# Later and paced first solve step, spread fetches of the compression weights, and a transposition by matmul, in a hybrid attention and RWKV-7 layer

## The chip, the core and the metric

The kernel runs on one core of a Trainium2 chip. The metric is the device time of one execution in microseconds (us). The kernel before takes 551.33 us, the median of 3 runs (551.25 to 551.44).

Five instruction streams run side by side, each in its own order: TensorE (PE, matmuls, with its weight loads as PEld), VectorE (DVE), ScalarE (ACT), GpSimd (POOL) and SyncE (SP), which here only issues DMA transfers. An instruction that waits for a semaphore holds up everything behind it on its engine.

## What is computed

One decoder layer for 256 tokens of width 2048. A normalised input goes through one wide projection, whose columns feed two groups of heads: eight heads of sparse attention (NSA) and sixteen heads of RWKV-7 (a recurrence over time with a 64x64 state per head). Both outputs are gated and go through one output projection. Cut to its frame, the reference reads:

```python
h      = rms_norm(x, pre_norm_g) @ w_in          # one projection, split by columns
kc     = compress(k_cmp, pos_k, k_w1, k_w2)      # 15 blocks of 32 tokens
vc     = compress(v_cmp, pos_v, v_w1, v_w2)
o_c    = softmax(q @ kc + bias) @ vc             # compressed branch
o_s, o_w                                         # selected and windowed branches
attn   = g0 * o_c + g1 * o_s + g2 * o_w
# RWKV-7, for every head and token
sa     = state @ a_t
state  = state * w_t + sa * b_t + v_t * k_t
y_t    = state @ r_t
out    = x + rms_norm((concat(attn * silu(za), y * silu(zb))) @ w_out)

def compress(kv, pos, w1, w2):
    flat = (blocks of 32 tokens of kv) + pos     # 32 x 128 = 4096 wide
    return silu(flat @ w1) @ w2
```

The layer is computed in float32 accuracy: each weight is split into a high and a low part of type f32r, a float32 that TensorE takes at a higher rate than plain float32.

## The kernel before

**Pieces.** The projection is cut into pieces of 128 output columns, which the main loop goes through one by one (L1251 and below). A piece j consists of two halves of 512 KB of weights. `load_raw` (L314) has SP fetch a half into one of four buffers; `cast` makes the high part on ACT (L322) and the low part on DVE (L323). Tiles carry the piece and the half: `rf170` is the raw first half of piece 17, `hf170` its high part and `lf170` its low part. (The profile leaves the number out and shows a serial number: `hf__1431` is `hf170`, `lf__1430` is `lf170`, `hf__1481` is `hf171`.) PE multiplies a half in 16 matmuls with the high part and 8 with the low one, all through the helper at L171. A weight buffer comes free when its cast is done, so a cast that is late on DVE holds up SP's next fetch and every DMA behind it.

**Order.** A planner in Python decides the order. Work beside the projection runs in lanes of generators; a `yield x` asks to go on x us of estimated PE time later. Tiles of SBUF come from a pool of 66 units (`arena`), PSUM from `banks`. Then the instructions are laid out by priority, and each engine runs in order. `pace(ins, to)` makes an instruction wait for a matmul on the chip; `behind` only fixes an order. `marks` holds the last matmul after each piece, so `marks[-1]` is the one after the newest piece.

**The RWKV solve** (`solve`, L805) runs once for each half of the RWKV heads. Four DMAs (L816) gather a matrix from the tile GR, which DVE writes at L779, into DRAM (`us`), and one DMA (L822) loads it as U. Then 31 steps on DVE follow, each a multiplication (L829) and an addition (L831), the first at `j == 31`.

**The compression** (`compress`, L1029) runs for the keys (kc) and the values (vc). Its first weight matrix, cw1, comes in eight parts of 512 KB, four for each; `fetch_cw` (L1020) takes four arena units for a part and has SP fetch it (L1026). Eight small fp32 matmuls use a part. DVE copies the sum out of PSUM (`csb`, L1061), and a small matmul of 32 columns on that copy (L1064) adds up the four 32-row groups. An activation and a second small product follow.

**The input for the later pieces** comes once more: `stage` loads the input in two transfers of 1 MB (L526) and scales it in eight DVE instructions each (L529).

**An attention head** (`nsa_head`, L1091) turns its probabilities by PE: six transpositions of 128x128 and two of the small tile `lcs` (L1164), all through the helper at L200 with the fp32 identity.

Of the kernel before, what the change touches and what calls it, by code (L numbers as in the profile page):

```python
# [11 lines left out]
F32 = mybir.dt.float32  # L12
F32R = mybir.dt.float32r
AF = mybir.ActivationFunctionType
ALU = mybir.AluOpType

P = 128
# [119 lines left out]
def hybrid_block(ctx: ExitStack, tc: tile.TileContext, xT, xtok, wfm, wtm, wout, vecs, gpost, lora, table,  # L137
# [28 lines left out]
    def mm(o, lhsT, rhs, **kw):  # L166
        n = 1
        for d_ in rhs.shape[1:]:
            n *= d_
        now[0] += n * (1 if rhs.dtype == F32R else 4) / 2400.0  # L170
        last[0] = PE.matmul(o, lhsT, rhs, **kw)  # L171

    last = [None]
# [24 lines left out]
    def transpose(o, i, idn):  # L198
        now[0] += 0.11
        PE.transpose(out=o, in_=i, identity=idn)  # L200
# [21 lines left out]
    def bank():  # L222
        while banks.find(1) is None:
            yield lambda: banks.find(1) is not None
        return banks.take(1)
# [210 lines left out]
    marks = []  # L436
# [45 lines left out]
    cmat = cst[:, K_CM:K_CM + P]  # L482
    bonr = cp.tile([P, P], F32R, name="bonr")
    ACT.activation(bonr, bones, AF.Copy)
    gmask = cst[:, K_GM:K_GM + P]
    qsum = cst[:, K_Q:K_Q + 32]
    smask = cst[:, K_SM:K_SM + T]
# [317 lines left out]
    def solve(hb):  # L805
# [16 lines left out]
        SP.dma_start(U, us)  # L822
        POOL.memset(Z, 0.0)
        POOL.memset(Zs[0:64, 0:1024:33], 1.0)
        yield 5.0
        for j in range(31, 0, -1):
            w = 32 - j
            t_ = tmp[0:64, 0:j * w].rearrange("p (s t) -> p s t", s=j)
            DVE.tensor_tensor(t_, U[:, 0:j, j:j + 1].to_broadcast([64, j, w]),  # L829
                              Z[:, j:j + 1, j:32].to_broadcast([64, j, w]), op=ALU.mult)  # L830
            DVE.tensor_tensor(Z[:, 0:j, j:32], Z[:, 0:j, j:32], t_, op=ALU.add)  # L831
            if hb == 0 or j % 2:
                yield ZLAT
# [195 lines left out]
    def compress(a, nm):  # L1029
        if a == 0:  # L1030
            pace(SP.dma_start(post, pos), marks[-2])
            pace(SP.dma_start(w2t, cw2), marks[-2])
            fetch_cw(2, False)
        blks = yield from sb(4)
        blk = blks.ap.rearrange("p (j g i) -> p j g i", j=32, g=2)
        POOL.memset(blk[:, :, :, 15:16], 0.0)
        src = cT[nm].ap
        for g in range(2):
            w_g = bass.AP(tensor=src.tensor, offset=src.offset + g * T, ap=[src.ap[0], [1, 32], [16, 15]])
            DVE.tensor_tensor(blk[:, :, g, 0:15], w_g, post[:, a, :, None].to_broadcast([P, 32, 15]), op=ALU.add)  # L1040
        cT[nm].free(2.0)
        yield 1.0
        cps = yield from bank()
        for hf in range(4):
            n = 4 * a + hf
            fetch_cw(min(n + 3, 8), False)
            if n not in cws:
                yield lambda: arena.find(4) is not None
                fetch_cw(n + 1, True)
                yield 4.0  # L1050
            w1 = cws.pop(n)
            for j in range(2):
                for q in range(4):
                    jj = 4 * j + q
                    mm(cps[32 * q:32 * q + 32, 0:P], blk[:, 8 * hf + jj].rearrange("p g i -> p (g i)"),
                       w1[:, jj * P:jj * P + P], start=hf == 0 and j == 0, stop=hf == 3 and j == 1)
            w1.free(1.0)
            yield CWLAT
        blks.free(1.0)
        csb = yield from sb()  # L1060
        DVE.tensor_copy(csb[:, 0:P], cps[:, 0:P])  # L1061
        cps.free(1.0)
        yps = yield from bank()
        mm(yps[:, 0:32], csb[:, 0:P], qsum, start=True, stop=True)  # L1064
        csb.free(1.0)
        yh = tp.tile([P, 32], F32, tag="yh", name=f"yh{nm}")
        DVE.tensor_scalar(yh, yps[:, 0:32], 0.5, None, op0=ALU.mult)
        yps.free(1.0)
        yt = tp.tile([P, 32], F32, tag="yt", name=f"yt{nm}")
        ACT.activation(yt, yh, AF.Tanh)  # L1070
        DVE.scalar_tensor_tensor(yh, yt, 1.0, yh, op0=ALU.add, op1=ALU.mult)
        yield 2.0
        ops = yield from bank()
        if a == 0:
            mm(ops[:, 0:32], w2t[:, a, :], yh, start=True, stop=True)
            for g in range(2):
                ACT.activation(KCH[:, g, 128:144], ops[:, 16 * g:16 * g + 16], AF.Copy)
                DVE.tensor_tensor(KCL[:, g, 128:144], ops[:, 16 * g:16 * g + 16], KCH[:, g, 128:144].bitcast(F32),
                                  op=ALU.subtract)
        else:  # L1080
            for g in range(2):
                mm(ops[0:16, g * P:(g + 1) * P], yh[:, 16 * g:16 * g + 16], w2t[:, a, :], start=True, stop=True)
            opv = ops[0:16, 0:2 * P].rearrange("p (g d) -> p g d", g=2)
            ACT.activation(vcS[0:16], opv, AF.Copy)
            ACT.activation(vcS[64:80], opv, AF.Copy)
            DVE.tensor_tensor(vcS[32:48], opv, vcS[0:16].bitcast(F32), op=ALU.subtract)
        ops.free(2.0)
        ready_kv[nm] = True
        yield 0.4

    def nsa_head(h, qts):  # L1091
# [70 lines left out]
        for j in range(6):  # L1162
            transpose(ptf[:, j * P:(j + 1) * P], lg[:, j * P:(j + 1) * P], ident)
        for i in range(2):  # L1164
            transpose(ctp[0:80, i * P:(i + 1) * P], lcs[:, i, :].bitcast(F32), ident)
        pT = lg
        cTt = tp.tile([P, T], F32R, tag="hr", name=f"cTt{h}", bufs=NHR)
        ACT.activation(cTt[0:80], ctp[0:80, 0:T], AF.Copy)
# [82 lines left out]
    for j, (nm, i) in enumerate(FM):  # L1251
        if j == N_PRE_TM:
            token_major()
        if j == N_SWITCH - 6:
            lanes["stage"].append(stage())
        until(lambda: arena.find(4) is not None)
        pt = proj(j)
        if j == 0:
            row_statistics()
        A = halves[i // 4] if nm in ("k", "r", "v") else None  # L1260
        if nm == "wa":
            wa = pick(arena, 1)
            shifted(pt, j, 24, wa[:])
            rw.append(wa_split(wa))
        elif nm == "k":
            h2 = (i % 4) // 2
            if i % 2 == 0:
                A.pair[h2] = pick(arena, 4)
                pv = A.pair[h2].ap.rearrange("p (a b t) -> p a b t", a=2, b=2)
                for q in range(2):  # L1270
                    A.ks[i % 4 + q], A.nrm[i % 4 + q] = pv[:, 0, q], pv[:, 1, q]
                A.left = getattr(A, "left", [2, 2])
            shifted(pt, j, i, A.ks[i % 4])
            rw.append(k_norm(A, i % 4, i))
            if i % 2 == 1:
                rw.append(k_ready(A, i % 4 - 1))
                if i % 4 == 1:
                    rw.append(begin(i // 4))
                for q in (i - 1, i):
                    lanes[f"blk{q % 2}"].append(block(A, i // 4, q % 4, q))  # L1280
        elif nm in ("r", "v"):
            o = pick(arena, 1)
            shifted(pt, j, (8 if nm == "r" else 16) + i, o[:])
            (A.r if nm == "r" else A.v)[i % 4] = o
        elif nm in ("kc", "vc"):
            if i == 0:
                cT[nm] = pick(arena, 2)
            with at("evac"):
                evacuate(cT[nm][:, i * T:i * T + T], pt, j)
            if i == 1:  # L1290
                lanes["nsa0"].append(compress(("kc", "vc").index(nm), nm))
        elif nm in ("ks", "kw"):
            kt = fbuf[turn[0] % 2][:, 1:T + 1]
            with at("evac"):
                evacuate(kt, pt, j)
            for o, w in ((slice(0, 128), slice(0, 128)), (slice(400, 528), slice(128, 256))) if nm == "ks" else (
                    (slice(144, 400), slice(0, 256)),):
                ACT.activation(KCH[:, i, o], kt[:, w], AF.Copy)
                DVE.tensor_tensor(KCL[:, i, o], kt[:, w], KCH[:, i, o].bitcast(F32), op=ALU.subtract)
        elif nm == "q":  # L1300
            qt = pick(arena, 1)
            with at("evac"):
                evacuate(qt[:], pt, j, SCALE)
            lanes[f"nsa{i % NL}"].append(nsa_head(i, qt))
        else:
            if i == 0:
                zt_ = rp.tile([P, 8 if nm == "za" else 4, T], F32, tag="lorS" if nm == "za" else "waS", name="all" + nm)
            if nm == "za" or i < 4:
                z = Kept(zt_[:, i, :])
            else:  # L1310
                z = pick(arena, 1)
            with at("evac"):
                evacuate(z[:], pt, j, 0.5)
            lanes["gate"].append(silu(i + (8 if nm == "zb" else 0), z))
            if nm == "zb":
                gates.append((i, z))
# [184 lines left out]
```

## Time and profile before

| quantity | value |
|---|---|
| median of 3 runs | 551.33 us |
| the profiled execution's own time | 553.0 us |
| span from its first to its last instruction | 551.2 us |
| mean TensorE clock granted in it | 0.994 |
| DVE, ACT, POOL busy in the span | 427.4, 312.2, 55.7 us |
| bytes moved | 101.98 MB, 185 GB/s on average |

Times in the rows of the profile count from the first instruction of the span. A row of the timeline holds its start, its length to the end of the last instruction in the group, engine, line, operation, tiles (written <- read), the count and, in brackets, the idle time before it and what ended it. Matmuls are pipelined, so the spacing of the starts tells what one costs, and the length of a single one does not. A plain fp32 matmul leaves two records.

### The profile page before, as it was taken

How to read it: one execution, taken by the hardware profiler on the slowest of the kernel's cores; microseconds unless marked ns; L12 is line 12 of the kernel's file. 1: busy time of each engine (PE TensorE's matmuls, PEld its weight loads, DVE VectorE, ACT ScalarE, POOL GpSimd, SP SyncE). 2: the span in 40 equal slices, each digit the busy share in tenths (PEclk: the TensorE clock that was granted, in tenths of full speed). 3: DMA queues.
4: the chain of work that ended last, by engine and by line, in shares of the span. 5: the costliest groups of instructions: out<-in, count | busy, mean ns of one | idle time of the engine just before them, and what ended most of it. 6: DMA issues, size and time to landing. Idle time of an engine off the chain costs nothing.

```text
span 551.2 us, 10942 instructions
## 1 busy us (share of the span) xinstructions
PE 541.9 (98%) x4208; PEld 483.8 (88%) x4208; DVE 427.4 (78%) x862; ACT 312.2 (57%) x595; POOL 55.7 (10%) x101
## 2 busy tenths in 40 slices
PE   9999999999999999999999999999999999999995
PEld 8999999989988888888998888988988887888884
DVE  5888999869989877556699969999776753776654
ACT  6858665432746554443766868758764434754532
POOL 3202433000000000000532101000000000000000
PEclk9999999998999999999999999999999999999998
DMA  8957444888555575433456464444642446847524
GB/s 298 386 186 262 142 156 155 316 267 319 168 187 182 189 223 182 141 107 99 117 184 203 132 175 141 149 156 134 183 131 86 155 165 205 317 154 230 190 77 152
DMA packets 41167, 101.98 MB, mean 185 GB/s; under 512 B 14203, under 2 KB 16412, under 8 KB 40476
## 3 DMA queue, kind: packets, MB, share of 16 engines
q1 hardware_dynamic: 40828, 100.98, 55.4%
q8 instruction: 33, 0.54, 0.4%
q10 hardware_dynamic: 288, 0.31, 0.2%
q14 instruction: 18, 0.15, 0.1%
HBM read 96.03 MB, written 5.24 MB: 184 GB/s over the span
## 4 chain that ended last, share of the span: by engine, by line
PE 88%; DMA 5%; ACT 2%; DVE 2%; SPq 1%; issue 1%; POOL 0%; DVEq 0%; ACTq 0%
PE banks L171 86%; PE banks L200 2%; DMA xr<-in_xT_dram 1%; DMA arena<-us 1%; DMA us<-GR 1%; DMA rf__3422<-in_wfm_dram 1%; DMA rf__95<-in_wfm_dram 1%; SPq L816 1%; ACT xs L397 0%; POOL arena L713 0%; ACT arena L499 0%; DVE arena L999 0%; ACT L712 0%; DVE GR L779 0%; DVE arena L733 0%
## 5 line engine op out<-in xcount | busy, mean ns | idle before, releaser
L171 PE MATMUL banks<-arena 128*32 128x128 f32 (+3 forms) x470 | 30.2, 253 | 1.1 <-POOL arena L304 1.1
L171 PEld LDWEIGHTS banks<-arena 128*32 128x32 f32 (+3 forms) x470 | 25.7, 136 | 4.5 <-POOL arena L304 1.1
L829 DVE TENSOR_TENSOR arena<-arena 64x31 f32<-64x31 f32 (+15 forms) x62 | 20.4, 329 | 5.2 <-DMA arena<-us 4.5
L831 DVE TENSOR_TENSOR arena<-arena 64x31 f32<-64x31 f32 (+15 forms) x62 | 20.3, 328 | 0.6
L633 ACT ACTIVATE small<-small 128x256 f32<-128x256 f32 x25 | 12.5, 502 | 10.7 <-DVE small L619 7.1
L618 ACT ACTIVATE small<-banks 128x256 f32<-128x256 f32 x37 | 13.9, 375 | 4.4 <-PE banks L171 4.3
L200 PE MATMUL banks<-small,arena 128*128 128x128 f32 x96 | 14.7, 274 | 0.0
L634 DVE SCALAR_TENSOR_TENSOR arena<-small 128x256 f32<-128x256 f32 x25 | 11.8, 476 | 3.6 <-ACT small L633 3.5
L678 DVE RECIPROCAL arena<-banks 128x256 f32<-128x256 f32 x8 | 13.8, 1740 | 0.8 <-PE banks L171 0.8
L1140 ACT ACTIVATE arena<-arena,mx 128x128 f32<-128x128 f32 (+1 forms) x32 | 14.1, 443 | 0.0
L171 PE MATMUL banks<-VS,GR 128*64 128x64 f32 x256 | 13.6, 228 | 0.0
L171 PEld LDWEIGHTS banks<-VS,GR 128*64 128x64 f32 x256 | 10.9, 137 | 1.5 <-issue 0.4
L713 POOL TENSOR_SCALAR arena<-arena 128x256 f32<-128x256 f32 x8 | 9.5, 1189 | 26.1 <-ACT arena L712 26.1
L952 POOL MEMSET arena<- 64x256 f32 x12 | 3.7, 308 | 83.4 <-DVE arena L634 28.8
L200 PEld LDWEIGHTS banks<-small,arena 128*128 128x128 f32 x96 | 11.2, 140 | 1.0
L779 DVE TENSOR_TENSOR GR<-banks,small 128x1024 f32<-128x1024 f32 x8 | 9.7, 1212 | 2.9 <-PE banks L171 2.9
L926 DVE COPY VS<-banks 64x512 f32<-64x512 f32 x8 | 5.5, 687 | 7.5 <-PE banks L171 7.5
L956 POOL TENSOR_TENSOR arena<-arena,PC 128x256 f32<-128x256 f32 x4 | 3.3, 836 | 78.7 <-DVE arena L946 49.7
L732 POOL TENSOR_SCALAR AR<-arena,small 128x4 f32<-128x4 f32 x8 | 7.4, 932 | 31.8 <-DVE arena L634 31.8
L1136 DVE CUSTOM_DVE_ANT_0 arena<-banks,arena 128x128 f32<-128x128 f32 (+1 forms) x32 | 10.0, 349 | 0.0
L171 PE MATMUL banks<-AR,arena 64*128 64x128 f32 x128 | 9.3, 285 | 0.0
L171 PEld LDWEIGHTS banks<-AR,arena 64*128 64x128 f32 x128 | 7.8, 187 | 1.5 <-issue 0.7
(1165 smaller groups left out, 1780.5 us busy)
## 6 DMA issues: line engine op xcount, KB each, us to landing
arena<-in_cw_dram SPq DMA_DIRECT2D x8, 512.0 KB, 8.2
arena<-in_wfm_dram SPq DMA_DIRECT2D x4, 512.0 KB, 8.6
arena<-in_xT_dram SPq DMA_DIRECT2D x2, 1024.0 KB, 7.5
xres<-in_xtok_dram SPq DMA_DIRECT2D x2, 1024.0 KB, 5.7
out_dram<-y SPq DMA_DIRECT2D x7, 256.0 KB, 2.4
xr<-in_xT_dram SPq DMA_DIRECT2D x3, 512.0 KB, 7.2
bscr<-arena SPq DMA_DIRECT2D x1, 1536.0 KB, 7.5
arena<-bscr SPq DMA_DIRECT2D x8, 128.0 KB, 2.9
```

The source lines that it names most:

```text
L171: last[0] = PE.matmul(o, lhsT, rhs, **kw)
L200: PE.transpose(out=o, in_=i, identity=idn)
L618: ACT.activation(t, pt[:, T:2 * T], AF.Copy, scale=scale)
L633: ACT.activation(tm, f[:, 0:T], AF.Copy, scale=vcol(V_MU, c))
L634: DVE.scalar_tensor_tensor(o, f[:, 1:T + 1], omu[:, c:c + 1], tm, op0=ALU.mult, op1=ALU.add)
L678: DVE.reciprocal(A.nrm[i], sp[:, :T])
L713: POOL.tensor_scalar(u[:], u[:], 1.0, None, op0=ALU.add)
L779: DVE.tensor_tensor(A.GR[:, i].rearrange("p h c t -> p (h c) t"), gp.ap.rearrange("p h (c t) -> p (h c) t", c=4), gmask[:, None, :].to_bro ...
L829: DVE.tensor_tensor(t_, U[:, 0:j, j:j + 1].to_broadcast([64, j, w]), Z[:, j:j + 1, j:32].to_broadcast([64, j, w]), op=ALU.mult)
L831: DVE.tensor_tensor(Z[:, 0:j, j:32], Z[:, 0:j, j:32], t_, op=ALU.add)
L1136: DVE.tensor_tensor_reduce(out=dst, in0=src, in1=bb, scale=1.0, scalar=-3.0e38, op0=ALU.add, op1=ALU.max, accum_out=mx[:, i, j:j + 1])
L1140: ACT.activation(dst, dst, AF.Exp, bias=mx[:, i, j:j + 1], accum_out=sm[:, i, j:j + 1])
```

## The change

The change has five parts.

- `idr`, a copy of the 128x128 identity of type f32r, is made once by ACT.
- In `solve` the planner is asked for 10 instead of 5 us of PE time before the loop, and the first multiplication of the loop is paced on `marks[-1]`.
- In `compress` the planner lets 2.5 us pass between the copy `csb` and the small matmul, and that matmul is ordered behind `marks[-1]`.
- In `nsa_head` the two transpositions of `lcs` (16 in all) become f32r matmuls with `idr` as the moving side, 128 columns each.
- At the pieces 8 to 16 the loop fetches one part of cw1 a piece, where at least 24 units of the arena are free.

```diff
+    idr = cp.tile([P, P], F32R, name="idr")
+    ACT.activation(idr, ident, AF.Copy)
@@ solve
-        yield 5.0
+        yield 10.0
         for j in range(31, 0, -1):
             w = 32 - j
             t_ = tmp[0:64, 0:j * w].rearrange("p (s t) -> p s t", s=j)
-            DVE.tensor_tensor(t_, U[:, 0:j, j:j + 1].to_broadcast([64, j, w]),
-                              Z[:, j:j + 1, j:32].to_broadcast([64, j, w]), op=ALU.mult)
+            step_ = DVE.tensor_tensor(t_, U[:, 0:j, j:j + 1].to_broadcast([64, j, w]),
+                                      Z[:, j:j + 1, j:32].to_broadcast([64, j, w]), op=ALU.mult)
+            if j == 31:
+                pace(step_, marks[-1])
@@ compress
         csb = yield from sb()
         DVE.tensor_copy(csb[:, 0:P], cps[:, 0:P])
         cps.free(1.0)
+        yield 2.5
         yps = yield from bank()
         mm(yps[:, 0:32], csb[:, 0:P], qsum, start=True, stop=True)
+        behind(last[0], marks[-1])
@@ nsa_head
         for i in range(2):
-            transpose(ctp[0:80, i * P:(i + 1) * P], lcs[:, i, :].bitcast(F32), ident)
+            mm(ctp[0:80, i * P:(i + 1) * P], lcs[:, i, :], idr, start=True, stop=True)
@@ loop over the pieces
+        if 8 <= j < 17 and arena.busy.count(False) >= 24:
+            fetch_cw(cwn[0] + 1, True)
```

What this does to the order of the instructions shows at three places. In the changed kernel the lines move by 2 to 8: L779 becomes L781, L816 L818, L822 L824, L829 L831, L831 L835, L1026 L1030 and L1061 L1065.

SP, before, from the fetch of three parts of cw1 to the one of the last two; `GR0`, `us0` belong to the first solve:

```order
L1026 DMA arena_73<-in_cw1_dram 128x1024 x3
L314 DMA rf170__1428<-in_wfm_dram 128x1024
L526 DMA arena_73<-in_xT_dram 128x2048
L314 DMA rf171__1478<-in_wfm_dram 128x1024
L1026 DMA arena_73<-in_cw1_dram 128x1024 x2
L816 DMA us0_1459<-GR0_675 32x16x32 x3
L314 DMA rf180__1521<-in_wfm_dram 128x1024
L816 DMA us0_1459<-GR0_675 32x16x32
L314 DMA rf190__1567<-in_wfm_dram 128x1024
L822 DMA arena_73<-us0_1459 64x1024
```

All eight parts are fetched here and in the four rows behind. The same stretch of SP in the changed kernel is without them; two come later, the last one here:

```order
L528 DMA arena_73<-in_xT_dram 128x2048
L314 DMA rf170__1434<-in_wfm_dram 128x1024
L314 DMA rf171__1483<-in_wfm_dram 128x1024
L818 DMA us0_1465<-GR0_677 32x16x32 x3
L314 DMA rf180__1523<-in_wfm_dram 128x1024
L818 DMA us0_1465<-GR0_677 32x16x32
...
L314 DMA rf211__1839<-in_wfm_dram 128x1024
L314 DMA rf220__1873<-in_wfm_dram 128x1024
L1030 DMA arena_73<-in_cw1_dram 128x1024
```

Six of the eight parts now stand ahead of these rows, between the fetches of the pieces 10 and 15. The first 1 MB of the second input stands ahead of piece 17. The eighth part of cw1 stands behind the fetch of `rf220`, which waits until DVE has cast `lf200`.

DVE, before, around the first step of the first solve (L829); L529 scales the second input, L1061 copies the compression's sum:

```order
L323 TENSOR_TENSOR lf170__1430<-rf170__1428,hf170__1431 128x1024
L616 SCALAR_TENSOR_TENSOR arena_73<-banks_74,small_72 128x256
L323 TENSOR_TENSOR lf171__1480<-rf171__1478,hf171__1481 128x1024
L1040 TENSOR_TENSOR arena_73<-arena_73,small_72 128x32x15
L829 TENSOR_TENSOR arena_73<-arena_73 64x31
L1061 COPY arena_73<-banks_74 128x128
```

The copy stands right behind the first step. In the changed kernel (L831 is the multiplication, L835 the addition):

```order
L531 SCALAR_TENSOR_TENSOR arena_73<-arena_73,small_72 128x256 x8
L794 TENSOR_TENSOR arena_73<-banks_74,arena_73 128x256
L781 TENSOR_TENSOR GR0_677<-banks_74,small_72 128x1024
...
L1044 TENSOR_TENSOR arena_73<-arena_73,small_72 128x32x15
L831 TENSOR_TENSOR arena_73<-arena_73 64x31
L835 TENSOR_TENSOR arena_73<-arena_73 64x31
L831 TENSOR_TENSOR arena_73<-arena_73 64x60
L835 TENSOR_TENSOR arena_73<-arena_73 64x30x2
L831 TENSOR_TENSOR arena_73<-arena_73 64x87
L1065 COPY arena_73<-banks_74 128x128
```

The scaling of the second input went ahead of the last writing of GR; before, it stood behind it. The cast of `lf171` went from ahead of the first step to behind it, four rows past the copy.

PE, before, around the small product (the row of 128x32); `xs0` and `xs1` are the input:

```order
L171 MATMUL banks_74<-xs1_76,hf161__1389 128x256 x11
L171 MATMUL banks_74<-xs1_76,lf161__1388 128x256 x8
L171 MATMUL banks_74<-xs0_75,hf170__1431 128x256 x3
L171 MATMUL banks_74<-small_72,arena_73 128x32
L171 MATMUL banks_74<-xs0_75,hf170__1431 128x256 x13
```

It stands three matmuls into piece 17. In the changed kernel it stands behind the whole of it, and the value compression (32x128) is cut in three:

```order
L171 MATMUL banks_74<-xs1_76,lf171__1485 128x256 x5
L171 MATMUL banks_74<-arena_73 32x128 x16
L171 MATMUL banks_74<-xs1_76,lf171__1485 128x256 x3
L171 MATMUL banks_74<-small_72,arena_73 128x32
...
L171 MATMUL banks_74<-xs0_75,hf210__1732 128x512 x4
L171 MATMUL banks_74<-arena_73 32x128 x8
L171 MATMUL banks_74<-xs0_75,hf200__1690 128x512 x4
```

The last eight small matmuls, which use the eighth part of cw1, now stand behind four matmuls each of the pieces 20 and 21; before, all 32 stood within piece 17.

## The prediction

> **What bounds the kernel now.** The page comes first, for the engine that sets the time.
>
> ```profile
> PE 541.9 (98%) x4208; PEld 483.8 (88%) x4208; DVE 427.4 (78%) x862; ACT 312.2 (57%) x595; POOL 55.7 (10%) x101
> ```
>
> PE is busy for 541.9 of 551.2 us. A change can gain only where PE idles, where its clock is low, or where matmuls become cheaper. I looked for the first two in PE's timeline: beside the two ends of the program, one stall stands out.
>
> ```profile
> 122.15 0.52 PE L171 MATMUL banks<-xs,hf__1431 128*128 128x256 f32 x3
> 124.44 0.41 PE L171 MATMUL banks<-small,arena 128*128 128x32 f32 x2 [1.78 <-DVE arena L1061]
> 124.69 3.02 PE L171 MATMUL banks<-xs,hf__1431 128*128 128x256 f32 x13
> 127.51 1.43 PE L171 MATMUL banks<-xs,lf__1430 128*128 128x256 f32 x8
> 128.78 2.08 PE L171 MATMUL banks<-xs,hf__1481 128*128 128x256 f32 x16
> 130.69 0.40 PE L171 MATMUL banks<-xs,lf__1480 128*128 128x256 f32 x2
> ```
>
> The compression's small product waits 1.78 us for the copy at L1061. Behind it the matmuls are slow: the 21 of `hf170` and `lf170` take 128.78 - 124.69 = 4.09 us, the 16 of `hf171` 130.69 - 128.78 = 1.91 us, or 0.119 each. At that pace 21 take 2.51 us, so 1.58 us go here. The windows of the trace tell why (length, busy time of PE, PEld, DVE, ACT and POOL, granted clock, DMA share and GB/s):
>
> ```profile
> 18.98:22.40 3.42, 2.80 (x24) 2.60 (x23) 3.42 (x6) 2.96 (x4) 0.00 (x0) 1.00 1.03 417
> 121.40:124.81 3.41, 1.63 (x14) 1.43 (x13) 0.75 (x5) 1.05 (x1) 0.00 (x0) 1.00 0.98 276
> 124.81:128.23 3.42, 3.42 (x18) 3.42 (x18) 3.28 (x10) 0.48 (x1) 0.00 (x0) 0.50 1.01 410
> 128.23:131.64 3.41, 3.41 (x48) 3.28 (x50) 3.31 (x9) 1.39 (x3) 0.00 (x0) 1.00 0.83 225
> ```
>
> After the window in which PE worked only 1.63 of 3.41 us the clock was 0.50 for one window. A stretch of the same length with 2.80 of 3.42 us busy (18.98 to 22.40) was followed by no such drop. So the stall costs 1.78 + 1.58 = **3.36 us**. The chain of waits and DVE's timeline show what it hangs on.
>
> ```profile
> 108.28 1.24 DVE GR L779
> 110.46 2.03 SPq L816
> 113.06 5.09 DMA us<-GR
> 118.24 5.73 DMA arena<-us
> ```
>
> ```profile
> 111.78 3.26 DVE L529 SCALAR_TENSOR_TENSOR arena<-arena,small 128x256 f32<-128x256 f32 x8 [0.80 <-DMA arena<-in_xT_dram]
> 118.47 1.22 DVE L323 TENSOR_TENSOR lf__1480<-rf__1478,hf__1481 128x1024 fp32r<-128x1024 f32 x1
> 123.99 0.20 DVE L829 TENSOR_TENSOR arena<-arena 64x31 f32<-64x31 f32 x1 [3.39 <-DMA arena<-us]
> 124.12 0.27 DVE L1061 COPY arena<-banks 128x128 f32<-128x128 f32 x1
> ```
>
> The copy stands on DVE behind the solve's first step, and that step waits for U, which lands at 123.97. DVE idles for 3.39 us with the copy ready to go.
>
> **The change part by part.** *The small product* moves behind `lf171`, where PE comes some 7 us later: from 122.15 on, 48 f32r matmuls of 0.119 us (5.7 us) and 16 small fp32 ones stand ahead of it. The copy still waits for U, but is done about a microsecond after it. Stall and slow window go: -3.36 us.
>
> *What is late next: U.* Call its landing L. GR is written later than before: the scaling (3.26 us by its row) now precedes it on DVE. By these rows the second input was fetched late, behind three of five parts of cw1:
>
> ```profile
> 98.51 1.60 SPq L1026 DMA_DIRECT2D arena<-in_cw_dram  x3
> 104.38 0.33 SPq L526 DMA_DIRECT2D arena<-in_xT_dram  x1
> 106.11 0.33 SPq L314 DMA_DIRECT2D rf__1478<-in_wfm_dram  x1
> 106.53 0.90 SPq L1026 DMA_DIRECT2D arena<-in_cw_dram  x2
> ```
>
> In the changed order its fetch stands ahead of piece 17's, and the parts are gone from here. DVE comes to it once it has cast `lf151`, whose buffer `rf__1478` takes at 106.11; I estimate that the input is there by then, 1.7 us after the old issue. Then GR is done at 106 + 3.3 + 0.4 (an estimate for one add of 256 columns) + 1.2 = 110.9, against 109.5 before. The last gather can go about 112.5, behind `rf180`, which waits for its buffer. From there I bound with two cases. As before, gather and load took 5.09 and 5.73 us. In the second solve, where the queue was quiet, from these rows:
>
> ```profile
> 324.40 1.95 SPq L816 DMA_DIRECT2D us<-GR  x4
> 328.05 0.47 SPq L822 DMA_DIRECT2D arena<-us  x1
> ```
>
> ```profile
> 333.23 0.20 DVE L829 TENSOR_TENSOR arena<-arena 64x31 f32<-64x31 f32 x1 [1.15 <-DMA arena<-us]
> ```
>
> the last of four gathers was issued at about 325.9 and all had landed by 328.05, and U was loaded by 333.2, 5.2 us on: 2.2 and 5.2 us. So L lies between 112.5 + 7.4 = 119.9 and 112.5 + 10.9 = 123.4. The five parts of cw1 that crowded the queue are gone; I take **L = 120.5**, near the quiet end.
>
> *Who waits for U.* The first step still holds DVE. Behind it now stand the copy, the cast of `lf171`, and all later casts. `lf171` is done 3.4 us after L (2.2 for eight steps and the copy, 1.2 for the cast), at 123.9; PE asks for it 40 matmuls after 122.15, at 126.9. That is covered. The pace on the first step waits for the key compression's eighth matmul. PE has 24 more of these and 34 f32r matmuls behind it before 122.15, so it comes by about 116.5, ahead of L, and costs nothing.
>
> *The eighth part of cw1* is covered less. It stands on SP behind the fetch of `rf220`, which waits for the cast of `lf200`:
>
> ```profile
> 142.16 1.21 DVE L323 TENSOR_TENSOR lf__1696<-rf__1694,hf__1697 128x1024 fp32r<-128x1024 f32 x1
> ```
>
> ```profile
> rf__1841<-in_wfm_dram SPq DMA_DIRECT2D x1, 512.0 KB, 4.8
> rf__1875<-in_wfm_dram SPq DMA_DIRECT2D x1, 512.0 KB, 4.5
> rf__1944<-in_wfm_dram SPq DMA_DIRECT2D x1, 512.0 KB, 3.7
> ```
>
> Before, that cast ended at 143.37, 19.4 us after U, and DVE hardly idled between (3.31 of 3.41 us busy in the window from 128.23). Now `lf171` is added (1.2) and about 0.8 of the value compression's DVE work has moved behind: 19.8 us after L. With 0.35 us for SP's issue and 4.5 us to land (these rows, of the same size and place), the part is there at L + 24.65 = 145.2. PE wants it, at full clock and with no wait, after 144 f32r matmuls of 256 columns (17.2 us), 8 of 512 (1.9), 24 small ones (1.6) and two small products (0.5): 122.15 + 21.2 = 143.3.
>
> ```profile
> 131.02 1.07 PE L171 MATMUL banks<-arena 128*32 128x128 f32 x30
> 132.03 0.41 PE L171 MATMUL banks<-yhkc,small 128*128 128x32 f32 x2
> 150.54 1.09 PE L171 MATMUL banks<-xs,hf__1737 128*128 128x512 f32 x4
> 151.47 1.11 PE L171 MATMUL banks<-xs,lf__1736 128*128 128x256 f32 x8
> ```
>
> (15 small ones in 1.01 us, four wide ones in 0.93.) PE loses 145.2 - 143.3 = **+1.85 us** there in all, part of it in shorter waits ahead for DVE's other results, so that I expect the last wait at about 1 us. With L and landing at their ends (3.7 to 4.8) it is +0.5 to +5.1.
>
> *Two lcs transpositions a head.*
>
> ```profile
> 364.38 0.38 PE L200 MATMUL banks<-small,lcs 128*80 128x128 f32 x2
> 364.51 0.60 PE L171 MATMUL banks<-xs,lf__4275 128*128 128x256 f32 x3
> 364.95 1.32 PE L171 MATMUL banks<-xs,hf__4330 128*128 128x512 f32 x5
> ```
>
> ```profile
> 276.38 0.61 PE L171 MATMUL banks<-small,arena 128*128 128x128 f32 x4
> 276.75 0.86 PE L171 MATMUL banks<-ht__3162,xs 128*128 128x268 f32 x5
> ```
>
> A pair and three f32r matmuls take 0.57 us, so the pair costs 0.57 - 0.36 = 0.21. No f32r matmul of under 256 columns runs in this trace. Half the columns at the f32r rate would be 0.06 each, 0.12 a pair: 8 x -0.09 = -0.7 us. Two fp32 matmuls (four records) took 0.37 us to the next start; the transpositions' own pair shows 0.13 there, and hands another 0.08 on, so I count 0.45: 8 x 0.24 = +1.9. Between these I take the nearest row, the f32r matmul of 256 columns, in full: 0.24 a pair, **+0.2 us**.
>
> *Edits at nothing.* `idr` is one ACT instruction at the start, where ACT waits for its inputs. The six early parts of cw1 (6 x 0.5 MB) go out between pieces 10 and 15, where PE never idled and ACT waited 1.1 us for one half at most; if that cover is gone, one half lands about 1.3 us later (0.5 MB at the 410 GB/s of the window above) and PE stalls for as much. Beyond 268 us, where the second RWKV half begins, matmuls on its matrices and the casts change places, and DVE has little room:
>
> ```profile
> 274.00:290.00 16.00, 16.00 (x128) 15.65 (x126) 15.25 (x31) 10.73 (x25) 6.87 (x9) 1.00 0.55 172
> ```
>
> It idled for 0.75 of 16 us and PE for none. One cast more ahead of what PE needs would be 1.2 us less those 0.75; I allow 0 to 1 us and take 0, since the work ahead of DVE there starts earlier too.
>
> **Sum.** Against the profiled execution (span 551.2 us, own time 553.0): -3.36 + 1.85 + 0.2 = -1.3 us. The median of the runs (551.33) lies 0.1 above the span, so I apply the difference to it: **550.0 us**.
>
> **A rule weighed.** By the trace, 1.78 us of idle time was followed by a halved clock. The Trainium skill, TensorE: Matmul & The Clock Gate, section "Why this matters for your kernels", says "No PE-idle gaps >~3µs between matmul bursts", and puts a drop behind one whole idle window. By that rule the stall would cost 1.78 us alone, and the sum would be about 0.3 us slower than before. The trace speaks against it here: a window 48% busy was enough.
>
> **The rivals.**
>
> *1. The slow clock comes back.* The wait for the eighth part is long enough for its window, and the 1.58 us return: 551.6. For it: no row tells where between 18% and 52% of idle time the limit lies. Against it: 1 us of 3.41 is 29%. 15%.
>
> *2. U comes late* (the slower side). One mechanism: each microsecond of L beyond 118.65 goes through the cast of `lf200` and SP's queue into the eighth part, and so to PE. It breaks even at L = 121.8 (-3.36 + 0.2 + L - 118.65 = 0) and is slower by over 0.2% from 122.9. For it: before, the gather and the load took 5.09 and 5.73 us. At L = 123.4 it gives 551.33 + 1.6 = 552.9. 17%.
>
> *3. f32r of 128 columns runs at the fp32 rate:* 1.9 in place of 0.2, 551.7. The kernel uses f32r only from 256 columns on, so no row decides it. 17%.
>
> *4. Nothing is late.* L at 119.9, the part landing in 3.7 us (+0.45) and the f32r matmuls at half the columns (-0.7): 547.7. 10%.
>
> *5. The clock drop was not the stall's doing*, as the rule above has it: -1.78 + 1.85 + 0.2, 551.6. The drop began at the first window's end after the stall and lasted one window, so 3%.
>
> *6. The change does not do what it says.* The pace may never bind, as worked out above, and two of eight parts still come late. This is in the forecast.
>
> **How the numbers follow.** The forecast of 550.0 has 38%, with its own range of 548.8 to 551.2 (L from 119.3 to 121.7). A measurement of this kernel tells 0.2%, 1.1 us, from no change: under 550.2 is faster, above 552.4 slower. Faster: somewhat over half of the forecast, rival 4, and some of 1 and 3 where U is early: 0.40. Slower: rival 2, and 1 and 3 where they meet each other or a late U: 0.24. Same: the rest, 0.36. The range of 8 in 10 reaches from 548.0 to 553.2: rival 4 half out below, rivals 2 and 3 together out above.
>
> **What would show it.** Right, step by step: no wait of PE for L1065 and clock 1.00 in all windows from 118 to 132; GR written at about 110.9, L at 119.9 to 121.5; DVE's first L831 waiting for `us`, not for PE; PE waiting about 1 us for cw1 at the last eight small matmuls near 144; a pair of lcs matmuls at about 0.24 us. Wrong: PE waiting for `lf171`, a second window at 0.50, lcs pairs at 0.45, or PE waiting for GR's successors after 268 us.

## The result and the profile after

| | median us (lowest to highest) | runs |
|---|---|---|
| before | 551.38 (551.25 to 553.09) | 4 |
| after | 558.27 (557.01 to 562.13) | 4 |

The ratio is 1.0119, with a 95% interval of 1.0083 to 1.0155: the changed kernel is slower by 4.6 to 8.5 us, outside the predicted range. The profiled execution of after took 562.13 us, the longest of its four; its span is 560.3 us and its mean granted clock 0.990 (the three others: 555.2 to 556.8 us at 0.996 to 0.999).

PE's timeline after shows three waits between 118 and 160 us, where before had one:

```profile
130.24 1.08 PE L171 MATMUL banks<-arena 128*32 128x128 f32 x32 [1.72 <-issue]
139.11 0.65 PE L171 MATMUL banks<-arena 128*32 128x128 f32 x16 [1.39 <-DMA arena<-in_cw_dram]
150.68 1.08 PE L171 MATMUL banks<-arena 128*32 128x128 f32 x16 [2.79 <-DMA arena<-in_cw_dram]
```

The wait of the small product is gone, as forecast. 5.90 us of other waits stand in its place, all of them at the small matmuls of the value compression. The first is put down to "issue": nothing in the row names what it waited for. DVE's timeline does:

```profile
107.35 3.26 DVE L531 SCALAR_TENSOR_TENSOR arena<-arena,small 128x256 f32<-128x256 f32 x8
110.86 1.22 DVE L781 TENSOR_TENSOR GR<-banks,small 128x1024 f32<-128x1024 f32 x1
122.74 0.21 DVE L831 TENSOR_TENSOR arena<-arena 64x31 f32<-64x31 f32 x1 [4.65 <-DMA arena<-us]
123.89 0.28 DVE L1065 COPY arena<-banks 128x128 f32<-128x128 f32 x1
129.18 0.96 DVE L1044 TENSOR_TENSOR arena<-arena,small 128x480 f32<-128x480 f32 x1
142.25 1.22 DVE L323 TENSOR_TENSOR lf__1689<-rf__1687,hf__1690 128x1024 fp32r<-128x1024 f32 x1
```

L1044 makes the second block of inputs for the value compression, and it ends at 130.14, 0.1 us ahead of PE's start. It stands on DVE behind seven steps of the solve (a multiplication and an addition each), the copy and two casts, and these stood still for 4.65 us until U came at 122.7. GR was done at 112.1, since the scaling L531 ran ahead of it. Yet U came 1.2 us earlier than in the kernel before (123.97). What is new is PE: without the stall it wants this block at 128.5. In the kernel before it came at 131.02, and the block (L1040 there) had been done since 128.85:

```profile
127.86 0.99 DVE L1040 TENSOR_TENSOR arena<-arena,small 128x480 f32<-128x480 f32 x1
```

SP's timeline of after has the other two waits:

```profile
112.10 1.41 SPq L818 DMA_DIRECT2D us<-GR  x3
114.08 0.44 SPq L818 DMA_DIRECT2D us<-GR  x1
119.21 0.50 SPq L824 DMA_DIRECT2D arena<-us  x1
131.95 0.43 SPq L1030 DMA_DIRECT2D arena<-in_cw_dram  x1
143.88 0.42 SPq L1030 DMA_DIRECT2D arena<-in_cw_dram  x1
```

In the chain of waits the same two parts, issue to landing, take:

```profile
131.95 7.12 DMA arena<-in_cw_dram
...
143.88 6.76 DMA arena<-in_cw_dram
```

Then the clock. The windows of after, with the columns as in the prediction:

```profile
146.49:149.90 3.41, 1.39 (x7) 0.80 (x5) 3.41 (x7) 2.23 (x5) 0.00 (x0) 1.00 0.86 318
149.90:153.31 3.41, 2.63 (x20) 1.93 (x21) 3.12 (x7) 0.00 (x0) 1.33 (x4) 0.50 0.55 186
153.31:156.72 3.41, 3.41 (x14) 3.02 (x13) 1.21 (x2) 1.36 (x2) 0.32 (x1) 0.50 0.01 2
412.71:416.13 3.42, 3.42 (x66) 2.66 (x64) 0.53 (x3) 1.79 (x6) 0.00 (x0) 1.00 0.32 104
416.13:419.54 3.41, 3.41 (x21) 2.79 (x11) 3.19 (x7) 1.27 (x4) 0.00 (x0) 0.50 0.02 5
```

The last wait halves the clock for two windows, in which PE was busy for 2.63 + 3.41 us; half of that, 3.0 us, is the most that they cost. A third slow window, at 416, follows one in which PE never idled.

Together: waits 5.90 - 1.78 = +4.1, clock 3.0 - 1.58 = +1.4 at most. So the first matmul of the first half of piece 28 starts 6.13 us later than before, 0.8 of it from ahead of 118 us:

```profile
192.83 1.55 PE L171 MATMUL banks<-xs,hf__2228 128*128 128x512 f32 x6
```

```profile
198.96 1.32 PE L171 MATMUL banks<-xs,hf__2226 128*128 128x512 f32 x5
```

(before, then after). The window at 416 adds up to 1.7 in this execution; about one more comes between 268 and 300, where PE waits 0.76 at 297.72 and 0.25 at 288.32.

### The profile page after: what moved, and what is told of

Its sections match the earlier page's. It is cut to its first block, busy times and chain, and to the rows that moved or that the text cites. A ratio compares the mean times of both kernels' runs of the same rounds, so it can differ in the third digit from the quotient of the medians.

```text
span 560.3 us, 10949 instructions
## 1 busy us (share of the span) xinstructions
PE 545.6 (97%) x4208; PEld 485.5 (87%) x4208; DVE 427.3 (76%) x862; ACT 311.6 (56%) x596; POOL 57.4 (10%) x101
## 4 chain that ended last, share of the span: by engine, by line
PE 87%; DMA 6%; ACT 3%; DVE 2%; issue 1%; POOL 1%; SPq 0%; ACTq 0%; POOLq 0%
PE banks L171 85%; DMA arena<-in_cw_dram 2%; PE banks L200 2%; DMA xr<-in_xT_dram 1%; DMA rf__3377<-in_wfm_dram 1%; DMA rf__95<-in_wfm_dram 1%; ACT xs L397 0%; POOL arena L715 0%; ACT arena L501 0%; POOL arena L718 0%; DVE arena L1003 0%; ACT L714 0%; DVE lf__1689 L323 0%; DVE lf__1650 L323 0%; ACT hf__3380 L322 0%
## 5 line engine op out<-in xcount | busy, mean ns | idle before, releaser
L831 DVE TENSOR_TENSOR arena<-arena 64x31 f32<-64x31 f32 (+15 forms) x62 | 20.4, 329 | 5.3 <-DMA arena<-us 4.6
L835 DVE TENSOR_TENSOR arena<-arena 64x31 f32<-64x31 f32 (+15 forms) x62 | 20.4, 329 | 0.6
L1146 ACT ACTIVATE arena<-arena,mx 128x256 f32<-128x256 f32 (+1 forms) x32 | 14.1, 442 | 0.0
L718 POOL TENSOR_SCALAR arena<-arena,small 128x256 f32<-128x256 f32 x8 | 8.6, 1077 | 23.3 <-ACT arena L716 23.3
L1142 DVE CUSTOM_DVE_ANT_0 arena<-banks,arena 128x256 f32<-128x256 f32 (+1 forms) x32 | 10.1, 349 | 0.0
L781 DVE TENSOR_TENSOR GR<-banks,small 128x1024 f32<-128x1024 f32 x8 | 9.7, 1215 | 0.4 <-PE banks L171 0.4
```

The lines of the kernel that those rows point to most:

```text
L781: DVE.tensor_tensor(A.GR[:, i].rearrange("p h c t -> p (h c) t"), gp.ap.rearrange("p h (c t) -> p (h c) t", c=4), gmask[:, None, :].to_bro ...
L831: step_ = DVE.tensor_tensor(t_, U[:, 0:j, j:j + 1].to_broadcast([64, j, w]), Z[:, j:j + 1, j:32].to_broadcast([64, j, w]), op=ALU.mult)
L1142: DVE.tensor_tensor_reduce(out=dst, in0=src, in1=bb, scale=1.0, scalar=-3.0e38, op0=ALU.add, op1=ALU.max, accum_out=mx[:, i, j:j + 1])
L1146: ACT.activation(dst, dst, AF.Exp, bias=mx[:, i, j:j + 1], accum_out=sm[:, i, j:j + 1])
```

## The experiments

Times are medians; every ratio is to runs of the kernel before on the same chip and in the same stretch (their medians lie between 552.3 and 552.9, so compare ratios, not times, with the table above).

| run | holds | us | ratio, 95% interval |
|---|---|---|---|
| e1 | all parts but the product's move | 558.43 | 1.0101 (1.0063 to 1.0139) |
| e2 | the product's move alone | 555.42 | 1.0056 (1.0029 to 1.0083) |
| e3 | all, 16 free units suffice for a fetch | 558.64 | 1.0100 (1.0060 to 1.0140) |
| e4 | e3, 18 us asked for ahead of the solve | 556.66 | 1.0078 (1.0054 to 1.0103) |
| e5 | the f32r transpositions alone | 550.99 | 0.9974 (0.9956 to 0.9992) |
| e6 | the early fetches alone | 555.81 | 1.0055 (1.0035 to 1.0076) |
| e7 | all parts but the early fetches | 556.23 | 1.0055 (1.0023 to 1.0087) |
| e8 | e5, and the copy `csb` on ACT | 551.55 | 0.9974 (0.9957 to 0.9991) |
| e9 | all, GR ahead of the scaling | 553.13 | 1.0012 (0.9995 to 1.0029) |
| e10 | e6, GR ahead of the scaling | 552.07 | 0.9991 (0.9976 to 1.0007) |
| e11 | e5, e10, fetches from 16 units, copy on ACT | 554.57 | 1.0033 (1.0008 to 1.0059) |
| e12 | e5, e10, eighth part asked for earlier | 553.75 | 1.0021 (1.0001 to 1.0041) |

### e1 and e2: the product's move, left out and alone

e1 is the changed kernel without these lines, e2 the kernel before with them alone:

```diff
+        yield 2.5
         yps = yield from bank()
         mm(yps[:, 0:32], csb[:, 0:P], qsum, start=True, stop=True)
+        behind(last[0], marks[-1])
```

> The changed kernel without its part on the compression (no 2.5 us ahead of the small product, no order behind the newest piece). Theory A: the loss is three waits of PE at the value compression (1.72 for its blocks, which DVE builds late because U holds it, 1.39 and 2.79 for the seventh and eighth part of cw1, which SP issues late) and the slow clock behind them (about 2.7). Without this part the 32 small matmuls stand together again and both parts are issued right behind piece 18; the small product again stands ahead of U and waits about 2.2 us, with one slow window (1.5). That gives 552 to 554. Theory B: the early fetches of six parts collide with the weights and cost the time. Then it stays at 557 to 558.

> The kernel before with only the part on the compression. Theory A: the value compression is cut in three and the parts seven and eight come late as in the changed kernel, so PE waits for cw1 twice, 3 to 5 us in all, and the small product does not wait: 553 to 558. Theory B (early fetches at fault): there are none, the stall of 3.36 us is gone, 548 to 549.

e1 came out at 558.43: without the move the loss is all there. Its PE timeline has the wait for the copy back, although U lands at 121.8, 2.2 us earlier than before. The product now stands 14 f32r matmuls earlier on PE, 13 matmuls into the second half of piece 16:

```profile
123.25 0.41 PE L171 MATMUL banks<-small,arena 128*128 128x32 f32 x2 [1.92 <-DVE arena L1065]
```

e2 lost as well, 555.42, with the three waits of after in smaller form:

```profile
128.22 1.08 PE L171 MATMUL banks<-arena 128*32 128x128 f32 x32 [0.76 <-issue]
137.70 0.65 PE L171 MATMUL banks<-arena 128*32 128x128 f32 x16 [1.65 <-DMA arena<-in_cw_dram]
148.00 0.64 PE L171 MATMUL banks<-arena 128*32 128x128 f32 x16 [1.65 <-DMA arena<-in_cw_dram]
```

In e2 nothing is fetched early, GR is written ahead of the scaling, and U lands at 123.4, 0.6 us earlier than before. So the three waits need no later U: the move, with a PE that no longer stalls, is enough.

So the move loses on its own, and so do the other parts without it. The move makes these waits possible: it has the planner cut the 32 small matmuls apart and put the last parts of cw1 further back on SP.

### e3 and e4: the parts earlier, then the step later too

```diff
-        if 8 <= j < 17 and arena.busy.count(False) >= 24:
+        if 8 <= j < 17 and arena.busy.count(False) >= 16:
```

e4 has `yield 18` for `yield 10.0` in `solve` besides.

> The changed kernel with 16 in place of 24 free units as the condition of the early fetch. The seventh part is then fetched ahead of piece 17 and the eighth behind piece 19's second half; the 32 small matmuls of the value compression stand together. Theory A: no wait for cw1 above 0.5 us, the wait for the blocks (1.7 us) stays, the clock drops once at most: 550 to 552. Theory B: one early fetch more, so 557 or above.

> As the run before it, and 18 in place of 10 us ahead of the solve's first step. On DVE that step then stands behind the copy of the sum, the blocks, and the casts of the pieces 17 to 19, so nothing of the compression waits for U. Theory A: no wait of PE above 0.3 us between 118 and 165, clock 1.00 there, 547.5 to 549. Theory B: 557 or above. Theory C (the solve's length sets the time later, for the second half of the heads): a new wait of PE behind 190 us, 551 or more.

e3 got rid of both waits for cw1 and gained nothing (558.64). The wait at the value blocks grew, and a new one came; PE and DVE:

```profile
131.28 1.96 PE L171 MATMUL banks<-arena 128*32 128x128 f32 x64 [2.46 <-issue]
142.79 2.08 PE L171 MATMUL banks<-xs,lf__1613 128*128 128x256 f32 x8 [3.99 <-DVE lf__1613 L323]
```

```profile
123.37 0.20 DVE L831 TENSOR_TENSOR arena<-arena 64x31 f32<-64x31 f32 x1 [6.03 <-DMA arena<-us]
...
137.85 1.68 DVE L531 SCALAR_TENSOR_TENSOR arena<-arena,small 128x256 f32<-128x256 f32 x4 [2.58 <-DMA arena<-in_xT_dram]
```

Here the second half of the second input holds DVE, and the cast of `lf181` stands behind its scaling. In e4 the step no longer holds DVE near 120 and the clock is 1.00 up to the last microseconds, but 1.44 us remain at the cast of `lf181`, and the second solve is late as well: between 440 and 466 PE waits over and over for the recurrence behind it, first with

```profile
441.78 0.75 PE L171 MATMUL banks<-arena,GR 32*32 32x32 f32 x64 [1.22 <-DMA arena<-zt]
```

The same `yield` serves both solves, and much of what it saves at the first is lost again at the second. e3 came out in theory B's range, though its two waits are not for cw1; e4 in theory C's, new wait included.

### e5, e6, e7: the other parts

e5 has the two changes with `idr`, e6 the two lines at the pieces 8 to 16, e7 all but those two.

> The kernel before with the lcs transpositions as f32r matmuls alone. Theory A (from the spacing of the starts in the changed kernel's trace, about 0.184 us a pair against 0.21 before): 8 pairs x -0.03 = -0.2 us, no wait beside the kernel before's own; 550.8 to 551.6, ratio 0.999 to 1.001. Rival B (f32r of 128 columns at the fp32 rate, 0.45 a pair): +1.9 us, 553.2, ratio 1.0035.

> The kernel before with the early fetches of cw1 alone. The first solve step, the copy behind it and the small product keep their places of the kernel before, but the scaling of the second input stands ahead of GR on DVE and the cast of lf171 behind the first step. Theory A (the early fetches have a cost of their own): PE waits about 1 to 2 us near 123 for the copy behind U (landing at 122.7 to 123.5) and again about 1 us near 140 for the cast of lf181; 554 to 558, ratio 1.005 to 1.012. Rival B (the early fetches are free or a gain, and the loss of the kernel without the product's move came from the solve's later start): U lands before 122.5, the stall of 1.78 us shrinks, 549.5 to 551.5, ratio 0.997 to 1.000.

> The changed kernel without the early fetches (solve, product and transposition only). Theory A (the product's move alone makes the loss near 130 to 150, and the early fetches, which move U's landing, only shift it): the three waits of the kernel with the product's move alone come back (about 0.8 near 128, 1.6 near 138, 1.8 near 146) and the second solve is a little later; 553 to 556.5, ratio 1.003 to 1.010. Rival B (the parts are needed together, so without the early fetches the gain of the removed stall shows): 548 to 550.5.

e5 rules out the fp32 rate. Its gain, 0.4 to 2.4 us by the interval, is more than the 0.2 expected; why is taken up below. e6 and e7 each lose 0.55%: the early fetches lose as much alone as the rest without them. e7 has the three waits of e2 again, as its theory A said. GR is done at 110.1, ahead of the scaling, and U still lands at 124.5:

```profile
124.49 0.21 DVE L831 TENSOR_TENSOR arena<-arena 64x31 f32<-64x31 f32 x1 [3.27 <-DMA arena<-us]
129.33 1.08 PE L171 MATMUL banks<-arena 128*32 128x128 f32 x32 [1.24 <-issue]
```

In e6 U lands at 123.3, 0.7 us earlier than before. PE waits at the product, which as in e1 stands 14 matmuls earlier:

```profile
124.74 0.41 PE L171 MATMUL banks<-small,arena 128*128 128x32 f32 x2 [2.48 <-DVE arena L1061]
```

### e8: the copy off DVE

```diff
-        DVE.tensor_copy(csb[:, 0:P], cps[:, 0:P])
+        ACT.activation(csb[:, 0:P], cps[:, 0:P], AF.Copy)
```

> The kernel before with the transpositions as f32r matmuls, and with the compression's copy out of PSUM (csb) on ACT in place of DVE, so that the small product no longer stands behind U's wait; the order of PE stays as before. Theory A (the 1.78 us of idle time and the slow clock behind it hang on the copy alone, and DVE's next results for PE, the value blocks and the key's second product, come within 1 us of their time): 548 to 550, ratio 0.994 to 0.998, clock 1.00 from 118 to 132, and a wait of at most 1 us near 127 to 130. Rival B (the wait only moves on: the value blocks and the second small product stand behind U on DVE too): a wait of 1.5 us or more near 127 to 130 with a slow window behind it, 550.5 to 552.5.

The stall at the product went, and a smaller one came 5 us later, at the value blocks behind U again. Its span has no slow window but the last:

```profile
129.60 0.41 PE L171 MATMUL banks<-arena 128*32 128x128 f32 x4 [0.80 <-issue]
```

Yet e8 is no faster than e5, which keeps the stall: the profiled gain is not in the medians.

### e9 and e10: GR ahead of the scaling

The changed kernel (e9) and the early fetches alone (e10), with the scaling of the second input's first half ordered behind the last writing of GR. Beside the lines that list the instructions which write GR (`wrote`), nothing else is edited:

```diff
             yield 4.0
+            if q == 0:
+                yield lambda: len(getattr(halves[0], "wrote", ())) == 4
             for k in range(8):
-                DVE.scalar_tensor_tensor(xv[:, k, :], ...
+                s_ = DVE.scalar_tensor_tensor(xv[:, k, :], ...
+                if q == 0:
+                    behind(s_, halves[0].wrote[-1])
```

> The changed kernel with one thing added: the scaling of the second input's first half is ordered behind the last writing of GR on DVE, as it stood in the kernel before (GR at about 110 in place of 112.1; all four gathers then go out ahead of the fetch of rf180 and U ahead of rf190). Theory A (U's landing, held up by the scaling ahead of GR and by the fetches between, drives the waits near 130 to 150): U lands by about 118 to 119, the value blocks' wait of 1.7 near 130 goes, and the two waits for cw1 (1.4 and 2.8) shrink to 1 or less each; 552 to 555. Rival B (the parts of cw1 are late by their place on SP and by the traffic, whatever U does): the waits near 139 and 150 stay at 1.4 and 2.8 or more; 556 to 558.

> The kernel before with the early fetches alone, and the scaling ordered behind the last writing of GR. Theory A (the early fetches cost nothing by themselves; their loss of about 3 us comes from GR and with it U being late): U by 118 to 119, the stall of 2.5 near 122 and the waits near 140 go; 548.5 to 551, ratio under 1.000. Rival B (the traffic or the later second half of the input costs, whatever U does): 553 to 556.

One order on DVE gives back most of the loss: 558.27 to 553.13 (ratio 1.0119 to 1.0012) with the whole change, 555.81 to 552.07 (1.0055 to 0.9991) with the early fetches alone. DVE and SP in e9:

```profile
109.89 1.23 DVE L785 TENSOR_TENSOR GR<-banks,small 128x1024 f32<-128x1024 f32 x1 [1.83 <-PE banks L171]
111.03 1.67 DVE L533 SCALAR_TENSOR_TENSOR arena<-arena,small 128x256 f32<-128x256 f32 x4
...
121.44 0.20 DVE L835 TENSOR_TENSOR arena<-arena 64x31 f32<-64x31 f32 x1
```

```profile
111.15 1.94 SPq L822 DMA_DIRECT2D us<-GR  x4
113.90 0.35 SPq L314 DMA_DIRECT2D rf__1523<-in_wfm_dram  x1
114.58 0.50 SPq L828 DMA_DIRECT2D arena<-us  x1
```

GR is 1 us earlier, but U's load is issued 4.6 us earlier: the gathers now pass the fetch of `rf180` together, where the last of them stood behind it. The first step no longer waits for U at all. The new order differs elsewhere too: the cast of `lf171` stands ahead of the first step, and only one cast, in place of two, stands between that step and the last block of the value compression, which is done at 126.7. PE keeps one of the three waits:

```profile
146.68 0.65 PE L171 MATMUL banks<-arena 128*32 128x128 f32 x16 [1.28 <-DMA arena<-in_cw_dram]
```

### e11 and e12: looking for a version that beats both

e12 differs from e10 by the transpositions and by

```diff
-            fetch_cw(min(n + 3, 8), False)
+            fetch_cw(min(n + 4, 8), False)
```

> Candidate for a version that beats both: the kernel before with the f32r transpositions, the early fetches (from 16 free units on), the scaling ordered behind GR, and the compression's copy on ACT; the product and the solve stay as before. Theory A: U by 119, no wait over 0.5 us between 118 and 150, clock 1.00 there; 547.5 to 550, ratio 0.991 to 0.997. Rival B (the second half of the input, or the key's second product, is the next to be late): waits of 1 us or more near 128 to 145; 550 to 553.

> The kernel with the early fetches and GR first, with the f32r transpositions, and with the last two parts of cw1 asked for together (four parts ahead in place of three), so that the eighth goes out behind the fetch of rf191 and not behind that of rf200. Theory A (the 1.83 us that PE still waited for cw1 near 130 there came from the eighth part's place on SP, issued at 125.85 and landed at 131.89): the wait falls under 0.5, 549 to 551, ratio 0.994 to 0.998. Rival B (the parts land later for the traffic, or the next result is late in its place): a wait of 1 us or more stays between 126 and 150; 551 to 553.

Both missed the gain that they were made for; in e12 rival B's wait came. e11 waits 0.62 us near 138 and meets two slow windows from 402 on. In e12 the wait for cw1 fell from 1.83 to 0.65, and the second input's second half came ahead of the copy and of the cast of `lf181` on DVE:

```profile
137.01 1.68 DVE L533 SCALAR_TENSOR_TENSOR arena<-arena,small 128x256 f32<-128x256 f32 x4 [4.50 <-DMA arena<-in_xT_dram]
```

```profile
140.90 0.41 PE L171 MATMUL banks<-small,arena 128*128 128x32 f32 x2 [2.44 <-DVE arena L1067]
```

Two versions beat both kernels, e5 and e8, at the same ratio; e5 is the smaller.

## Why the prediction was wrong

**The step that failed is "Who waits for U".** It listed the copy and the casts behind the first solve step and found them covered. It left out L1044, the next block of the value compression, which stands on the same queue and which PE wants 6 us after U: 1.72 us. The prediction took the stall off in full, and did not ask of this block whether it is ready when PE comes 3.36 us sooner. e2 shows this: the move alone, U no later than in the kernel before, and PE waits 0.76 us for the same block. (In after the cast of `lf171` stands ahead of it as well.) In e9, with U and the casts earlier, the block is done 2.3 us ahead of PE and the wait is gone.

**U's landing** was taken as 120.5 and came at 122.7, inside its bounds. GR was done 1.2 us later than estimated, and the last gather, behind `rf180`, took until 119.2. Rival 2 had the right direction: at this L its formula gives +0.9 us, 552.2. It priced U's landing by one path to PE, where there were three.

**The eighth part of cw1** was the right place and the wrong size. The cast of `lf200` ended 20.7 us after U, against 19.8, and the part took 6.8 us to land, against 4.5 taken from weight fetches of the same size. PE waited 2.79 us there, against about 1. The seventh part was not in the sum at all (1.39 us, 7.1 us from issue to landing). The term of +1.85 measured +4.2, and with L1044 +5.9. In e2 and e7, without early fetches, both parts cost PE 1.65 to 1.83 each. In e9 the eighth still costs 1.28: its place on SP is late even when U is not.

**The slow clock came back**, which was rival 1 at 15%, and for two windows in place of one. With the third one near 416 it takes back more than the stall's 3.36 us had promised, in the profiled execution; the three others, with a mean clock of 0.996 to 0.999, lost less to it.

**That gain of 3.36 was also too large for the median.** 1.58 of it is the slow window of one profiled execution. Whether a stall is followed by one turns in part on where it falls. Windows in which PE was busy for 0.68 (e12), 1.39 (after), 1.49 (e1), 1.63 (before) and 1.76 us (e7) were each followed by a clock of 0.50. One of e3, busy for 1.65 us (127.17 to 130.58), was not, so busy time alone does not decide it. e6's wait of 2.48 us was not followed by one either; it fell across the end of a window (at 123.15):

```profile
119.74:123.15 3.41, 2.53 (x22) 2.32 (x20) 0.00 (x0) 1.06 (x1) 0.00 (x0) 1.00 0.75 215
123.15:126.57 3.42, 1.83 (x15) 1.83 (x16) 3.08 (x11) 0.95 (x1) 0.00 (x0) 1.00 0.46 175
126.57:129.98 3.41, 3.41 (x31) 3.41 (x30) 3.31 (x12) 1.41 (x3) 0.00 (x0) 1.00 0.72 248
```

In e5's profile the stall was 1.35 us, its window 2.06 us busy, and no slow window followed. Over the runs beside e5 to e8, 3 of 31 executions of the kernel before had a mean clock of 0.999 or more, and 6 of 12 of e5. That fits a gain of about one slow window in some executions over the 0.2 us of the transpositions. But a mean clock also holds the half-rate stretch at the program's end (before: from 548.07 on), and what shortened the stall was not tested, so the cause of e5's gain stays open. e8's profile loses no window there, yet five of its 12 executions have a mean of 0.994 or less. The prediction also took 0.2% as what a measurement can tell, from three runs; beside e5 to e8 the kernel before ranged from 551.03 to 557.86 us.

The Trainium skill, TensorE: Matmul & The Clock Gate, section "Part 1: The HAM clock gate (the "warmup" mystery)", says that the window is 3413 ns long and free-running. The trace agrees: changes of the clock lie whole multiples of 3.413 us apart (before: 124.81, 128.23, 548.07). Its limit of one whole idle window is not what the runs show: a window busy for 1.76 of 3.41 us (e7) was enough.

**The transpositions** were counted at +0.2 us. In after a pair and two f32r matmuls take 328.06 - 327.63 = 0.43 us:

```profile
327.63 0.29 PE L171 MATMUL banks<-idr,lcs 128*80 128x128 f32 x2
327.76 0.46 PE L171 MATMUL banks<-hr,bonr 128*128 128x256 f32 x2
328.06 0.60 PE L200 MATMUL banks<-small,arena 128*128 128x128 f32 x4
```

Less 2 x 0.119 this is 0.19 a pair, against 0.21 before: about -0.2 us in all. Rival 3 falls.

**Right** were: the wait for the copy gone, the pace without effect (L831 waited for `us`), and about 1 us of waits at most beyond 268. The size there was partly luck: the larger wait (0.76) was for ACT, not for a cast on DVE.

**Edits at nothing** was wrong for the early fetches. They drew the second input forward and with it the scaling ahead of GR. The prediction saw that and priced it as a part of L, not as the loss of the change: e9 against after is 5 to 6 us (558.27 to 553.13; 1.0119 to 1.0012). This is what the order is worth once the early fetches are in. It is not the price of a U later than in the kernel before: after and e6 have U earlier than that, and e7 loses 0.55% with the scaling behind GR. Nor is their traffic shown to be free. e10 comes out even (0.9991), but there U lands at 119.9, 4.1 us earlier than before, the stall is gone, and PE waits 1.83 us for cw1 instead. And the half that lands late, which the prediction named and took as nothing, is in the traces. PE takes 20.0 us over the same matmuls from 69 to 89 us in each of the five profiles without early fetches, and 0.2 to 0.9 us more in eight of the nine with them (0.5 in after, none in e4). In e9 ACT waited 3.02 us for a half fetched behind a part of cw1, and PE for what ACT does behind its cast:

```profile
73.53 0.39 PE L171 MATMUL banks<-hr,bonr 128*128 128x256 f32 x1 [0.63 <-ACT hr L672]
```

The solve's part was not run alone. With U in time, the parts on the solve, the compression and the transpositions together cost about 1 us, by e9 against e10; the intervals of the two overlap.

## What to carry to other kernels

Before you count a stall's removal as a gain, move its engine forward by as much and ask of everything that it reads next whether it is ready by then. For a wait at the head of an in-order queue, that means listing what stands behind it on that queue and following each entry to its reader; here the loss was not at the first one. Ask of an instruction that is free on its own engine what it now runs ahead of: here one ordering edge, which put 3.3 us of scaling back behind one write to GR, was worth over 5 us. Count a slow window that stands in one profile only by its share of the executions.

## What the runs showed of the hardware

In the windows of 3.41 us near the waits between 118 and 150, a clock of 0.50 followed PE's busy times of 0.68 to 1.63 and of 1.76 us, and did not follow 1.65 (e3), 1.83 (e6), 2.06 (e5) and 2.13 us (e9). So the change comes near half a window, but no single limit of busy time fits these traces. There is an exception that idle time doesn't explain: in after, e1, e2 and e5, slow windows between 402 and 420 follow windows in which PE was busy throughout. These hold the small 32x32 and 64-column matmuls of the recurrence, and the same stretch passes without a drop in other executions. Whether such matmuls count as low activity was not tested.
